# Where the second half's weight and activation tiles lie in SBUF, modulo 512 bytes

## The chip, the cores and the metric

The kernel runs on one core of a Trainium2 chip. The metric is the device time of one execution in microseconds; a profiled execution also leaves a trace with the start and length of each instruction on every engine: TensorE (PE, with its weight loads listed apart as PEld), VectorE (DVE), ScalarE (ACT), GpSimd (POOL) and SyncE (SP, which issues most DMAs).

## The reference, cut to what matters

Two transformer blocks run over 256 tokens of 1024 features, all in float32. The first block mixes, routes each token to two of 32 experts, and normalises. The second block has two layers; each is a feed-forward part, a mixer with two kinds of attention, and another feed-forward part:

```python
def _swiglu(h, w_gate_up, w_down):
    g, u = jnp.split(h @ w_gate_up, 2, axis=-1)
    return (jax.nn.silu(g) * u) @ w_down

for layer in range(DEPTH_2):                       # DEPTH_2 = 2, D_FF = 2816
    x = x + FFN_RES_WEIGHT * _swiglu(_rmsnorm(x, ffn1_norm[layer]), ...)
    x = x + _hybrid_mixer(_rmsnorm(x, mix_norm[layer]), w_in[layer], ...)
    x = x + FFN_RES_WEIGHT * _swiglu(_rmsnorm(x, ffn2_norm[layer]), ...)
return _rmsnorm(x, final_norm)
```

## The kernel before, in words

The second half (the second block, from about 698 us on) is what the change touches. Its weights stream from HBM into nine slots of 128 partitions x 8 KB (`Stream`). The `Feeder` takes half a slot at a time and splits it in two parts: ScalarE writes `hi`, the weight rounded to float32r (line 139), and VectorE writes `lo`, what is left of it (line 152). Each part is a tile of 128 x 1024 float32r, 4096 bytes in a partition. The two parts of one half slot are called a pair here. Six pairs exist (`HB3 = 6`); `fd.pair` hands out the next one, and a pair is written again when TensorE is done with it.

Activations are split in the same way, into tiles of 8192 bytes in a partition: `XH`, `XL` hold the normalised input, `OH`, `OL` the middle of a feed-forward part or the heads' outputs. A product is three matmuls, hi times hi, hi times lo and lo times hi (`mm3`, lines 284 to 287). Each matmul has its own weight load: one operand is loaded into the array first, 128 columns of 4 bytes (512 bytes in a partition; called stationary), the other is streamed past it (called moving). The trace writes `out<-moving,stationary`. There are three kinds in the second half:

- `block` in `ffn` and `feat_block` in `mixer`: the weight part is stationary, the activation tile is moving, 256 columns wide (`o<-XH,whi`). One block is 4 pairs x 24 = 96 matmuls.
- `down` in `ffn`, `skew_last` and the output projection: `OH` or `OL` is stationary, the weight part is moving, 512 columns wide (`g<-whi,OH`). One `down` is 2 pairs x 12 = 24 matmuls.
- `skew_first` and `tok_block`: `XH` or `XL` is stationary, the weight part is moving, 512 columns wide (`g<-whi,XH`).

One step of a feed-forward part is a block and a `down`, so six pairs, and there are 11 such steps in a part. The order of all work is written out by hand.

Tiles of a pool lie one after another in the order in which their tags appear. The two tags of the pool `w3` (line 1309) have six buffers of 4096 bytes each, all multiples of 512, so every weight part starts at one place modulo 512; call it 0. Behind it the pool `work3` begins with a tile of 112 floats (448 bytes, `pad0`) that nothing uses, then `XH`, `XL`, then one of 16 floats (64 bytes, `pad1`), then `OH`, `OL`. So the X tiles start at 448 and the O tiles at 0. Slices of 128 columns move by 512 bytes, and slices of the X and O tiles by 1024 or 512, so these places hold for every matmul.

In the first half, in one pool (`mid`), the tiles `OA`, `OB` and the weight tiles `w` are all 8192 bytes, so they start at one place modulo 512, and so do the nine slots.

Of the kernel before, what the change touches and what calls it, by code (L numbers as in the profile page):

```python
# [10 lines left out]
F32 = mybir.dt.float32  # L11
F32R = mybir.dt.float32r
# [166 lines left out]
def body(tc, A, out, taps=None, stop=None):  # L179
# [3 lines left out]
    with es:  # L183
# [20 lines left out]
        fd = Feeder(nc, st)  # L204
# [91 lines left out]
        def halves(p, names):  # L296

            return [p.tile([128, 8, 256], F32R, name=n, tag=n, bufs=1) for n in names]
# [50 lines left out]
        work = mpool = mid.enter_context(tc.tile_pool(name="mid", bufs=1))  # L349
# [18 lines left out]
        work = p1.enter_context(tc.tile_pool(name="work1", bufs=2))  # L368
        XH, XL = halves(const, ("XH", "XL"))
# [352 lines left out]
        for gi in range(2):  # L722
            for hf in range(2):
                banks = feat_block()
                for c in range(4):
                    n = 4 * hf + c
# [580 lines left out]
        p3 = ExitStack()  # L1307
        HB3 = fd.hb = 6
        w3 = p3.enter_context(tc.tile_pool(name="w3", bufs=fd.hb))
        fd.pair = lambda i: [w3.tile([128, 1024], F32R, name=n) for n in ("whi", "wlo")]  # L1310
        work = p3.enter_context(tc.tile_pool(name="work3", bufs=2))
        fd.order += order2

        work.tile([128, 112], F32, name="pad0", bufs=1)
        XH, XL = halves(work, ("XH", "XL"))
        work.tile([128, 16], F32, name="pad1", bufs=1)
        OH, OL = halves(work, ("OH", "OL"))
        xn = [work.tile([128, 1024], F32, name=f"xn{t}", bufs=1) for t in range(2)]
        junk = work.tile([128, 1024], BF16, name="junk", bufs=1)
        RS = [work.tile([128, 8], F32, name=f"rs{t}", bufs=1) for t in range(2)]  # L1320
# [589 lines left out]
```

## Time and profile before

| | us |
|---|---|
| median of 3 runs | 1706.86 (1705.93 to 1706.91) |
| profiled execution, own time | 1707.14 |
| its span, first to last instruction | 1705.3 |
| PE busy in the span | 1566.1 (92%) |
| PE weight loads busy | 1227.6 (72%) |
| DVE busy | 814.7 (48%) |
| ACT busy | 646.9 (38%) |

The trace gives a matmul's length with its way through the array, so matmuls overlap, and the pace is read from start to start. The granted clock is the share of 2.4 GHz that TensorE got in a stretch.

### The profile page before, as it was taken

To read this page: it belongs to the slowest core of one execution; us is meant where nothing else is said; L and a number is where in the kernel's file an instruction comes from. 1 tells how busy PE (TensorE), PEld (TensorE's weight loads), DVE (VectorE), ACT (ScalarE), POOL (GpSimd) and SP (SyncE) were. 2 spreads that over 40 slices of the span, in tenths; PEclk is the share of its full clock that TensorE was granted. 3 is DMA by queue.
4 is the path that set the end of the run, shared out by engine and by line. 5 is a ranking of instruction groups with operands and counts; after the bars stand their busy time and mean duration, and the time that the engine had idled before them with its cause. 6 is when DMAs were issued, how large, how long until landed. Compare 5 with 4: busy or idle time off the path is not lost.

```text
span 1705.3 us, 24578 instructions
## 1 busy us (share of the span) xinstructions
PE 1566.1 (92%) x10196; PEld 1227.6 (72%) x10196; DVE 814.7 (48%) x1202; ACT 646.9 (38%) x959; POOL 124.7 (7%) x153
## 2 busy tenths in 40 slices
PE   8799997777687876899999999999999999999998
PEld 7789972222222221599989879999899989889997
DVE  5765560000000000765567866555655567765554
ACT  6456420000000100444445655444544455654443
POOL 3430020000000100200003000000000021000000
PEclk9899999988988899899999999999999999999999
DMA  9756679999999999775514555555555514465510
GB/s 335 181 182 240 268 303 420 422 421 421 421 422 420 419 420 376 282 285 185 196 50 161 179 213 198 188 198 177 188 192 195 176 51 158 175 240 192 184 64 26
DMA packets 85893, 418.91 MB, mean 246 GB/s; under 512 B 7552, under 2 KB 7752, under 8 KB 49936
## 3 DMA queue, kind: packets, MB, share of 16 engines
q1 hardware_dynamic: 82112, 407.07, 63.3%
q0 software_dynamic: 3392, 9.17, 2.1%
q8 instruction: 82, 1.34, 0.3%
q10 hardware_dynamic: 272, 1.05, 0.2%
q14 instruction: 35, 0.29, 0.0%
HBM read 414.60 MB, written 2.62 MB: 245 GB/s over the span
## 4 chain that ended last, share of the span: by engine, by line
PE 55%; DVE 3%; DMA 1%; ACT 0%; issue 0%; POOL 0%; POOLq 0%; DVEq 0%; SPq 0%; ACTq 0%
PE g L285 8%; PE g L286 8%; PE g L287 8%; PE o L287 5%; PE o L285 5%; PE o L286 5%; PE a L285 4%; PE a L286 4%; PE a L287 4%; DMA slot<-in_w_down_dram 1%; DVE wlo L152 1%; PE tp L1355 1%; PE fo L1733 0%; PE t L1622 0%; DVE slot L1769 0%
## 5 line engine op out<-in xcount | busy, mean ns | idle before, releaser
L152 DVE TENSOR_TENSOR wlo<-slot,whi 128x1024 fp32r<-128x1024 f32 x298 | 360.3, 1225 | 234.3 <-ACT whi L139 234.0
L139 ACT ACTIVATE whi<-slot 128x1024 fp32r<-128x1024 f32 x300 | 311.2, 1055 | 257.1 <-PE o L286 83.2
L285 PE MATMUL o<-XH,whi 128*128 128x256 f32 x640 | 180.0, 281 | 0.0
L286 PE MATMUL o<-XL,whi 128*128 128x256 f32 x640 | 179.8, 281 | 0.0
L287 PE MATMUL o<-XH,wlo 128*128 128x256 f32 x640 | 179.8, 281 | 0.0
L285 PE MATMUL g<-whi,OH 128*128 128x512 f32 x416 | 165.5, 398 | 0.0
L287 PE MATMUL g<-whi,OL 128*128 128x512 f32 x416 | 162.1, 390 | 0.0
L286 PE MATMUL g<-wlo,OH 128*128 128x512 f32 x416 | 162.0, 390 | 0.0
L285 PE MATMUL a<-XH,whi 128*128 128x256 f32 x512 | 143.9, 281 | 0.0
L286 PE MATMUL a<-XL,whi 128*128 128x256 f32 x512 | 143.9, 281 | 0.0
L287 PE MATMUL a<-XH,wlo 128*128 128x256 f32 x512 | 143.9, 281 | 0.0
L1078 DVE TENSOR_TENSOR eb<-eb,eu 128x512 f32<-128x512 f32 x8 | 5.5, 688 | 259.5 <-PE eu L1074 249.8
L287 PEld LDWEIGHTS o<-XH,wlo 128*128 128x128 f32 x640 | 122.3, 191 | 0.0
L286 PEld LDWEIGHTS o<-XL,whi 128*128 128x128 f32 x640 | 120.6, 188 | 0.6
L285 PEld LDWEIGHTS o<-XH,whi 128*128 128x128 f32 x640 | 120.3, 188 | 0.6
L285 PE MATMUL g<-XH,whi 128*128 128x256 f32 x384 | 113.9, 297 | 0.0
L286 PE MATMUL g<-XL,whi 128*128 128x256 f32 x384 | 106.7, 278 | 0.0
L287 PE MATMUL g<-XH,wlo 128*128 128x256 f32 x384 | 106.7, 278 | 0.0
L287 PEld LDWEIGHTS a<-XH,wlo 128*128 128x128 f32 x512 | 98.3, 192 | 0.0
L286 PEld LDWEIGHTS a<-XL,whi 128*128 128x128 f32 x512 | 96.1, 188 | 0.6
L285 PEld LDWEIGHTS a<-XH,whi 128*128 128x128 f32 x512 | 96.1, 188 | 0.6
L1077 ACT ACTIVATE eb<-eg 128x512 f32<-128x512 f32 x8 | 4.8, 597 | 236.9 <-PE eu L1074 197.3
(520 smaller groups left out, 3469.6 us busy)
## 6 DMA issues: line engine op xcount, KB each, us to landing
slot<-in_gu_dram SPq DMA_DIRECT2D x79, 1024.0 KB, 4.9
slot<-in_w_gate_up_dram SPq DMA_DIRECT2D x45, 1024.0 KB, 19.8
slot<-in_dn_dram SPq DMA_DIRECT2D x40, 1024.0 KB, 5.0
slot<-in_w_in_dram SPq DMA_DIRECT2D x37, 1024.0 KB, 5.2
slot<-in_w_down_dram SPq DMA_DIRECT2D x31, 1024.0 KB, 19.8
ew<-in_w_gate_up_dram SPq DMA_DIRECT2D x31, 1024.0 KB, 19.8
e<-in_w_gate_up_dram SPq DMA_DIRECT2D x15, 1024.0 KB, 19.9
ew<-in_w_down_dram SPq DMA_DIRECT2D x14, 1024.0 KB, 19.8
```

What stands on the lines that cost most here:

```text
L139: self.nc.scalar.activation(hi[:, c], src[:, c], AF.Copy)
L152: self.low.tensor_tensor(lo[:, c], src[:, c], hi.bitcast(F32)[:, c], ALU.subtract)
L285: mm(o, sh, mh, start=start, stop=False, skip_group_check=skip)
L286: mm(o, sh, ml, start=False, stop=False, skip_group_check=skip)
L287: mm(o, sl, mh, start=False, stop=stop, skip_group_check=skip)
L1077: act(esg, g, AF.Silu)
L1078: dve.tensor_tensor(esg, esg, u, ALU.mult)
L1355: nc.tensor.transpose(p[:, i * 128:(i + 1) * 128], src[:, c], ident)
```

## The change

It changes where tiles start and nothing else: no instruction is added, removed or moved. In the pool `w3` each of the six pairs gets tags of its own, and unused tiles ("step") are placed between them: 32 floats (128 bytes) before pair 0, 16 floats (64 bytes) before each other pair, and 16 behind the last. Modulo 512, with 0 as above, pair 0 starts at 128, pair 1 at 192, then 256, 320, 384 and 448. The steps add up to 128 + 5 x 64 + 64 = 512 bytes, as `pad0` and `pad1` did, so `work3` starts at 0 again; its pads are gone, and `XH`, `XL`, `OH`, `OL` all start at 0. Pair `i % 6` is the `i`-th one that the Feeder fills; before, the pool rotated through its six buffers in the same way.

```diff
         w3 = p3.enter_context(tc.tile_pool(name="w3", bufs=fd.hb))
-        fd.pair = lambda i: [w3.tile([128, 1024], F32R, name=n) for n in ("whi", "wlo")]
+        HIGH_LOW = ("whi", "wlo")
+
+        for i in range(HB3):
+            w3.tile([128, 16 if i else 32], F32, name="step", tag=f"step{i}", bufs=1)
+            for n in HIGH_LOW:
+                w3.tile([128, 1024], F32R, name=n, tag=f"{n}{i}", bufs=1)
+        w3.tile([128, 16], F32, name="step", tag="step", bufs=1)
+        fd.pair = lambda i: [w3.tile([128, 1024], F32R, name=n, tag=f"{n}{i % HB3}", bufs=1) for n in HIGH_LOW]
         work = p3.enter_context(tc.tile_pool(name="work3", bufs=2))
         fd.order += order2
-
-        work.tile([128, 112], F32, name="pad0", bufs=1)
-        XH, XL = halves(work, ("XH", "XL"))
-        work.tile([128, 16], F32, name="pad1", bufs=1)
-        OH, OL = halves(work, ("OH", "OL"))
+        XH, XL, OH, OL = halves(work, ("XH", "XL", "OH", "OL"))
```

## Rows read from the trace of the kernel before

**Rows 1.** Page, part 1: busy us and share of each engine.

```profile
PE 1566.1 (92%) x10196; PEld 1227.6 (72%) x10196; DVE 814.7 (48%) x1202; ACT 646.9 (38%) x959; POOL 124.7 (7%) x153
```

**Rows 2.** A window of the second half: busy us (instructions) by engine, granted clock, DMA.

```profile
1000.00:1200.00 200.00, 199.40 (x1357) 183.37 (x1357) 115.42 (x124) 90.63 (x105) 2.63 (x5) 1.00 0.57 199
```

**Rows 3.** Waits of PE, 800 to 1705 us: total us, times, longest.

```profile
PE tp L1355 <- DVE xn L1348: 1.4, 5, 0.3
```

**Rows 4.** Groups by form, PE, 690 to 1705 us: shape, count, busy us, mean ns.

```profile
L285 PE MATMUL o<-XH,whi 128*128 128x256 f32 x640 | 180.0, 281 | 0.0
L285 PE MATMUL g<-whi,OH 128*128 128x512 f32 x416 | 165.5, 398 | 0.0
L285 PE MATMUL a<-XH,whi 128*128 128x256 f32 x512 | 143.9, 281 | 0.0
L286 PE MATMUL g<-XL,whi 128*128 128x256 f32 x384 | 106.7, 278 | 0.0
L285 PE MATMUL g<-whi,XH 128*128 128x512 f32 x64 | 27.1, 424 | 0.0
L285 PE MATMUL o<-whi,XH 128*128 128x512 f32 x64 | 27.1, 423 | 0.0
```

**Rows 5.** Tile whi, 800 to 1705 us: duration ns min/median/max.

```profile
L285 PE MATMUL o<-XH,whi x561: 281/281/281, 800.0 to 1681.4; 128*128 128x256 f32 x187
L285 PE MATMUL a<-XH,whi x448: 281/281/281, 811.5 to 1664.6; 128*128 128x256 f32 x150
L286 PE MATMUL g<-XL,whi x352: 276/276/283, 903.1 to 1536.2; 128*128 128x256 f32 x176
L287 PE MATMUL g<-whi,OL x384: 388/389/398, 806.5 to 1697.8; 128*128 128x512 f32 x192
```

**Rows 6.** Timeline, PE: start us, length; first and 97th matmul of a run.

```profile
1105.44 0.28 PE L285 MATMUL o<-XH,whi 128*128 128x256 f32 x1
...
1116.75 0.39 PE L285 MATMUL g<-whi,OH 128*128 128x512 f32 x1
```

**Rows 7.** Timeline, PE: first and 43rd matmul of a run.

```profile
1027.03 0.28 PE L287 MATMUL g<-XH,wlo 128*128 128x256 f32 x1
...
1031.79 0.28 PE L287 MATMUL g<-XH,wlo 128*128 128x256 f32 x1
```

**Rows 8.** Timeline, PE, first half: first and 97th matmul of a run.

```profile
197.40 0.28 PE L285 MATMUL o<-OB,w 128*128 128x256 f32 x1
...
208.92 0.40 PE L285 MATMUL g<-w,Y 128*128 128x512 f32 x1
```

**Rows 9.** Timeline, PE: first and 24th matmul of a `down`.

```profile
1100.00 0.39 PE L285 MATMUL g<-whi,OH 128*128 128x512 f32 x1
...
1105.21 0.39 PE L287 MATMUL g<-whi,OL 128*128 128x512 f32 x1
```

**Rows 10.** Timeline, PE: first and 19th matmul of a run in `skew_first`.

```profile
1022.09 0.39 PE L287 MATMUL o<-whi,XL 128*128 128x512 f32 x1
...
1026.21 0.39 PE L287 MATMUL o<-whi,XL 128*128 128x512 f32 x1
```

**Rows 11.** Groups by form, ACT and DVE, 800 to 1705 us.

```profile
L139 ACT ACTIVATE whi<-slot 128x1024 fp32r<-128x1024 f32 x265 | 275.4, 1055 | 234.3 <-PE o L286 74.4 <-PE a L286 72.6 <-issue 39.4
L152 DVE TENSOR_TENSOR wlo<-slot,whi 128x1024 fp32r<-128x1024 f32 x266 | 321.4, 1223 | 214.5 <-ACT whi L139 214.2
```

**Rows 12.** Timeline, PE, experts: three matmuls at once; then a group by form.

```profile
686.22 0.60 PE L1096 MATMUL ey<-slot,eb 128*32 128x512 f32 x3
...
L1603 PE MATMUL ro<-slot,eXH 128*128 128x512 f32 x16 | 8.2, 591 | 0.0
```

**Rows 13.** Groups by form, PEld, 790 to 1705 us: weight loads of 128 and 64 columns.

```profile
L285 PEld LDWEIGHTS o<-XH,whi 128*128 128x128 f32 x576 | 108.1, 188 | 0.6
L1735 PEld LDWEIGHTS fo<-PT,slot 128*64 128x64 f32 x32 | 3.9, 137 | 2.2
```

**Rows 14.** Timeline, PEld: a weight load beside the matmul that starts with it.

```profile
1105.44 0.19 PEld L286 LDWEIGHTS o<-XL,whi 128*128 128x128 f32 x1
```

## The prediction

> **What bounds the kernel now.** I read the page's engine totals first: PE is busy for 1566.1 us of the 1705.3 us span, and no other engine passes half [rows 1]. A window of the second half then shows PE busy for 199.4 of 200 us at the full granted clock of 1.00 (2.4 GHz) [rows 2], and the list of PE's waits there has little in it: its longest total is 1.4 us [rows 3]. So in the stretch that the change touches, the end is set by the pace of the matmuls alone. Nothing else there matters unless it makes PE wait.
>
> The pace has to be read from start to start. The same three-matmul product with the same tiles runs at two paces. A whole feed-forward block takes 1116.75 - 1105.44 = 11.31 us for 96 matmuls, 117.8 ns each [rows 6]. A run of 42 in the block of step 1, same shapes and places, takes 4.76 us, 113.3 ns each [rows 7]. The lengths mark the two: 281 ns goes with 117.8, 276 ns with 113.3. In the banks `o` and `a` every one is 281 (minimum, median and maximum agree); in `g` the median is 276 [rows 5]. A third pace stands in the first half, where moving tile and weight part start at one place: 11.52 us for 96, 120.0 ns [rows 8]. The reader is to see that these are steady states, constant over whole runs, with no wait in them and the clock at full.
>
> The wide matmuls have two: with O stationary and the weights at the same place, 23 starts in 5.21 us, 226.5 ns [rows 9]; with X stationary, 64 bytes before the weights, 18 in 4.12 us, 228.9 ns [rows 10]. Each matmul runs beside the weight load of the next, which starts with it [rows 14].
>
> **The change part by part.** No instruction goes, comes or moves, and no DMA or queue is touched. What changes is the distance, modulo 512, between the two tiles that PE reads at once. Weight part minus X is 64 now; it becomes 128, 192, 256, 320, 384 or 448 by pair. Weight part minus O is 0; it becomes the same six. None of these stands in the trace of before, so each cost is bounded by the nearest rows.
>
> (a) *256-wide, weights stationary.* There are 3 x (640 + 512 + 384) = 4608 [rows 4]. In `g` the mean of 278 lies 2/5 of the way from 276 to 281, so some 3/5 of 1152, 690, are at 113.3 and the other 3918 at 117.8. Lower bound: all come to 113.3, 3918 x 4.5 ns = -17.6 us. Upper bound: all come to 120.0, 3918 x 2.2 + 690 x 6.7 = +13.2 us. The value I take: all at 117.8, so +690 x 4.5 ns = +3.1 us. My reason: a moving tile passes 1024 bytes while the weight load passes 512, so modulo 512 the one overtakes the other once in each matmul. At distances 0 and 64 this falls near the start or the end, where the load has not begun or is done; there a clean state (113.3) exists beside a hindered one. At 128 to 448 it falls in the middle of the load each time, so I expect the hindered state always, at the price that the blocks show for it today.
>
> (b) *512-wide, O stationary.* 3 x 416 = 1248 [rows 4]. They leave distance 0 for six others. The one other distance with rows is that of X, 228.9: +2.4 ns x 1248 = +2.9 us, and that I take. Lower bound 0: the shortest length is 388 against a median of 389 [rows 5], so nothing faster is there to go to. Upper bound: the longest length is 398, +9 ns each, +11.2 us.
>
> (c) *512-wide, X stationary.* 3 x (64 + 64) = 384 [rows 4], already in the hindered state; 0.
>
> (d) *Filling the pairs.* A part of whi takes 1055 ns and of wlo 1223 ns, six pairs in a step of 11.3 + 5.4 = 16.7 us: 6 x 1223 = 7.3 us of DVE. ACT's wait before it ends mostly with PE freeing a pair, DVE's with ACT [rows 11]: the fillers wait for PE. If another place made these longer, half a step of slack hides it. Cost 0; they would show only if both doubled.
>
> Sum: 3.1 + 2.9 = +6.0 us on the profiled execution's own 1707.14 (span 1705.3 and 1.8 around it), 1713.1; the median of the runs lies 0.28 lower, so I say 1713. The bounds together: -17.6 to +24.4 on the median, 1689 to 1731.
>
> **The rivals.** *Clean everywhere (faster).* Whatever makes 117.8 of 113.3 needs the two tiles close together, within 64 bytes; from 128 on it is gone. For it: the pace is worst at distance 0 (120.0 [rows 8]), less at 64 (117.8 [rows 6]), and the change keeps exactly these two out. Against it: at 64 both states exist [rows 5], so distance alone doesn't decide. Time: -17.6 + 0 to 2.9, about 1691. It decides if the overtaking in the middle of a load costs nothing.
>
> *Place doesn't set the pace (no change).* The states come from how each run is entered: after `down` without a stall the blocks are at 117.8, after a stall often at 113.3. For it: the experts' matmuls read three slots at the same place at once, and all take 0.60 us, against 591 ns for one such matmul alone [rows 12], so reading at one place need not hurt. Against it: 120.0 and 226.5 each belong to one distance. Time 1707. The Trainium skill states such a rule: "TensorE: Matmul & The Clock Gate", section "Step-by-step: what each phase is for", says that streaming and weight loads have independent read ports, so loading doesn't take bandwidth from the running matmul, and "SBUF — State Buffer", section "SBUF: two separate sides", that PE never waits on anyone. By these the time would stay at 1707; the experts' rows agree, the three paces at one clock and one shape are not explained by them.
>
> *The reader gets stuck behind the load (much slower).* If the moving tile cannot overtake but follows the load until that ends, it runs at the load's rate. Loads of 128 and 64 columns take 188 and 137 ns [rows 13], 0.80 ns a column, so 102 ns for 128 where the moving tile needs 57. That is up to 45 ns lost, half of it over the six distances: 23 ns x (4608 + 1248) = +135 us, 1842. It decides as soon as the meeting place lies well inside the load. Against it: at distance 64, where the meeting comes early, the cost today is 4.5 ns, not 40.
>
> **How the numbers follow.** Forecast (hindered everywhere, +3 to +24 us, own range 1709 to 1731): 0.44. Clean everywhere, 1691: 0.32. No effect, 1707: 0.18. Stuck, 1842: 0.06. The range 1690 to 1731 leaves out the stuck case and the edges. About 0.2% (3.4 us) is what a measurement can tell from no change. Faster: 0.32. Slower: 0.06 and 0.40 of the forecast's 0.44, 0.46. Same: 0.22.
>
> **What would show it.** In the profile after, the lengths of `o<-XH,whi` and `a<-XH,whi`: 281 (forecast, no effect), 276 (clean), 283 or more (upper bound), above 300 (stuck). The median of `g<-XL,whi` should go from 276 to 281, and that of `g<-whi,OH` from 389 to about 392. The lengths should differ between runs of 24 by their pair: six pairs pass in each step, so a feed-forward part uses the same four for every block and the same two for every `down`. The first half must keep its times, and PE's waits must stay near 1.4 us; if they grow, step (d) is wrong. The prediction is wrong if blocks fall below 11.2 us or if the two halves' paces don't move at all.

## The result and the profile after

The changed kernel takes 1716.38 us (median of 4 runs, 1715.06 to 1717.82); the kernel before took 1706.39 beside it (4 runs, 1705.35 to 1706.91). The ratio is 1.006, 95% interval 1.0042 to 1.0077: slower by about 10 us. The profiled execution took 1716.62, its span 1714.8.

First the page's engine totals (busy us, share, instructions), then the window from 1000 to 1200 us (busy us of PE, PEld, DVE, ACT, POOL, then granted clock, DMA share, GB/s), then PE's longest wait from 800 to 1705 us (total, times, longest). They answer to [rows 1 to 3].

```profile
PE 1577.6 (92%) x10196; PEld 1234.1 (72%) x10196; DVE 815.0 (48%) x1202; ACT 646.8 (38%) x959; POOL 124.8 (7%) x153
```

```profile
1000.00:1200.00 200.00, 199.50 (x1349) 182.25 (x1348) 115.27 (x123) 90.89 (x105) 2.63 (x5) 1.00 0.58 202
```

```profile
PE tp L1358 <- DVE xn L1351: 1.2, 5, 0.3
```

PE is busy 11.5 us longer with the same 10196 instructions, and its weight loads (PEld), which run beside the matmuls, 6.5 us longer; the other engines are where they were. The clock in the window is still 1.00, and PE's longest total wait is 1.2 us. So the change is in the pace of the matmuls. The groups by form (shape, count, busy us, mean ns, idle before) and, for the tile `whi`, the durations (min/median/max ns) answer to [rows 4, 5]:

```profile
L285 PE MATMUL o<-XH,whi 128*128 128x256 f32 x640 | 180.0, 281 | 0.0
L286 PE MATMUL g<-XL,whi 128*128 128x256 f32 x384 | 107.8, 281 | 0.0
L285 PE MATMUL g<-whi,OH 128*128 128x512 f32 x416 | 167.0, 401 | 0.0
L285 PE MATMUL g<-whi,XH 128*128 128x512 f32 x64 | 27.2, 426 | 0.0
```

```profile
L285 PE MATMUL o<-XH,whi x562: 276/280/287, 799.8 to 1690.5; 128*128 128x256 f32 x188
L285 PE MATMUL a<-XH,whi x448: 276/280/287, 811.7 to 1673.6; 128*128 128x256 f32 x150
L286 PE MATMUL g<-XL,whi x352: 274/281/287, 904.4 to 1544.1; 128*128 128x256 f32 x176
L287 PE MATMUL g<-whi,OL x380: 388/394/404, 806.6 to 1704.6; 128*128 128x512 f32 x190
```

The one length 281/281/281 of before has become a spread from 276 to 287: the matmuls no longer run at one pace. The mean of `o` is even the same as before (281). Lengths with one minimum, median and maximum marked a steady state; a spread has to be read from start to start. Here is one step of the second feed-forward part, the first start of each pair's run (start us, length):

```profile
1103.43 0.40 PE L285 MATMUL g<-whi,OH 128*128 128x512 f32 x1
1106.19 0.40 PE L285 MATMUL g<-whi,OH 128*128 128x512 f32 x1
1108.96 0.28 PE L285 MATMUL o<-XH,whi 128*128 128x256 f32 x1
1111.81 0.28 PE L285 MATMUL o<-XH,whi 128*128 128x256 f32 x1
1114.63 0.29 PE L285 MATMUL o<-XH,whi 128*128 128x256 f32 x1
1117.49 0.28 PE L285 MATMUL o<-XH,whi 128*128 128x256 f32 x1
1120.31 0.40 PE L285 MATMUL g<-whi,OH 128*128 128x512 f32 x1
```

The `down` takes 1108.96 - 1103.43 = 5.53 us for 24, 230.4 ns each, where 226.5 stood before [rows 9]. The block takes 11.35 us for 96, 118.2 ns, where 117.8 stood [rows 6]. Within it the four pairs take 2.85, 2.82, 2.86 and 2.82 us. They are pairs 4, 5, 0 and 1, at distances 384, 448, 128 and 192: every second one is slower. The next steps of this part repeat these four paces. In the fourth part the blocks use pairs 0 to 3, and there the last pair, at 320, is faster than any of these. Its first start and the start of the next `down` are:

```profile
1620.53 0.28 PE L285 MATMUL o<-XH,whi 128*128 128x256 f32 x1
1623.25 0.39 PE L285 MATMUL g<-whi,OH 128*128 128x512 f32 x1
```

That is 2.72 us for 24, or 113.3 ns each, the fast pace of [rows 7]; in the first part the pair at 320 runs at 117.9.

The first half keeps its pace, 207.94 - 196.42 = 11.52 us for the 96 matmuls of [rows 8], and so do the fillers of [rows 11]:

```profile
196.42 0.28 PE L285 MATMUL o<-OB,w 128*128 128x256 f32 x1
...
207.94 0.40 PE L285 MATMUL g<-w,Y 128*128 128x512 f32 x1
```

```profile
L139 ACT ACTIVATE whi<-slot 128x1024 fp32r<-128x1024 f32 x265 | 275.4, 1055 | 241.5 <-PE o L286 74.4 <-PE a L286 72.6 <-issue 43.3
L152 DVE TENSOR_TENSOR wlo<-slot,whi 128x1024 fp32r<-128x1024 f32 x266 | 321.4, 1223 | 221.9 <-ACT whi L139 221.6
```

**All kinds over the whole second half.** For each kernel I took the mean of the intervals from one matmul's start to the next, over all recorded ones, without those interrupted by a stall (over 135 ns in blocks, 245 ns in the wide ones). Before and after: blocks 117.11 and 118.19 ns, downs 227.35 and 231.75, X stationary 229.67 and 232.01. The sum: 4608 x 1.08 + 1248 x 4.40 + 384 x 2.34 ns = 5.0 + 5.5 + 0.9 = 11.4 us, as much as PE's busy time rose. Between the first X-stationary matmul of the second half and the start of the last run of downs lie 983.2 us before and 993.2 after, 10.0 more; the two profiled executions differ by 9.5 in all. The last run of 72 downs, with 71 intervals, lies behind that stretch and adds 0.4 (71 x 5.5 ns), and the first half was 0.9 shorter in the profile after: 10.0 + 0.4 - 0.9 = 9.5. That leaves 1.0 us of the 11.4 that did not reach the end. Some 0.6 us of it are the 120 interrupted intervals and the matmuls of other kinds in the stretch, which together took 111.7 us before and 111.1 after. The rest is mostly that the sum counts the interrupted intervals at the full difference.

### The profile page after: what moved, and what is told of

It is laid out like the page before. It is cut to its first block, busy times and chain, and to the rows that moved or that the text cites. A ratio compares the mean times of both kernels' runs of the same rounds, so it can differ in the third digit from the quotient of the medians.

```text
span 1714.8 us, 24578 instructions
## 1 busy us (share of the span) xinstructions
PE 1577.6 (92%) x10196; PEld 1234.1 (72%) x10196; DVE 815.0 (48%) x1202; ACT 646.8 (38%) x959; POOL 124.8 (7%) x153
## 4 chain that ended last, share of the span: by engine, by line
PE 56%; DVE 3%; DMA 1%; ACT 0%; issue 0%; POOL 0%; POOLq 0%; DVEq 0%; SPq 0%; ACTq 0%
PE g L285 8%; PE g L287 8%; PE g L286 8%; PE o L287 5%; PE o L285 5%; PE o L286 5%; PE a L285 4%; PE a L287 4%; PE a L286 4%; DMA slot<-in_w_down_dram 1%; DVE wlo L152 1%; PE tp L1358 1%; PE fo L1736 0%; PE t L1625 0%; DVE slot L1772 0%
## 5 line engine op out<-in xcount | busy, mean ns | idle before, releaser
L139 ACT ACTIVATE whi<-slot 128x1024 fp32r<-128x1024 f32 x300 | 311.3, 1055 | 265.0 <-PE o L286 83.2
L286 PEld LDWEIGHTS o<-XL,whi 128*128 128x128 f32 x640 | 120.3, 188 | 0.8
```

What stands on the lines that cost most here:

```text
L139: self.nc.scalar.activation(hi[:, c], src[:, c], AF.Copy)
L286: mm(o, sh, ml, start=False, stop=False, skip_group_check=skip)
```

## The experiments

All kernels below have the instructions of the kernel before, in the same order; only tile places differ. "W - X, W - O" are the distances from X and O up to the weight part, in bytes. The paces are the means defined above; "second half" is the stretch from its first X-stationary matmul to the start of the last downs. The time of one execution also holds a first half that these edits don't touch and that ended between 693.8 and 698.3 us in the profiles, so it moves by some 4 us for reasons of its own; the paces and the second half are the better measure.

| kernel | W - X, W - O | time us | kernel before, beside it | blocks ns | downs ns | X stat. ns | second half us |
|---|---|---|---|---|---|---|---|
| before | 64, 0 | 1706.39 | | 117.11 | 227.35 | 229.67 | 983.2 |
| after | 128 to 448 | 1716.38 | 1706.39 | 118.19 | 231.75 | 232.01 | 993.2 |
| u128_64 | 128, 64 | 1718.16 | 1705.13 | 119.61 | 229.55 | 232.32 | 997.2 |
| u192_128 | 192, 128 | 1713.42 | 1705.13 | 117.37 | 233.11 | 233.00 | 990.8 |
| u256_192 | 256, 192 | 1723.76 | 1705.13 | 119.73 | 233.44 | 228.75 | 1001.2 |
| u320_256 | 320, 256 | 1706.08 | 1705.13 | 117.11 | 227.37 | 229.68 | 983.2 |
| alt256 | 64 / 320, 0 / 256 | 1704.04 | 1704.62 | 117.10 | 227.39 | 229.72 | 983.1 |
| f96_32 | 96, 32 | 1719.08 | 1704.62 | 118.69 | 233.08 | 233.28 | 996.6 |
| f288_224 | 288, 224 | 1715.53 | 1704.62 | 118.33 | 233.28 | 233.21 | 995.5 |
| f160_96 | 160, 96 | 1727.21 | 1704.62 | 119.97 | 233.38 | 233.72 | 1002.9 |
| alt128 | 64 / 192, 0 / 128 | 1693.94 | 1707.10 | 113.68 | 230.66 | 231.25 | 971.2 |
| x128_o0 | 128, 0 | 1717.95 | 1707.10 | 119.69 | 228.67 | 232.58 | 996.6 |
| hilo | whi 64, 0; wlo 128, 64 | 1716.49 | 1707.10 | 118.19 | 231.75 | 231.67 | 993.0 |
| two128 | four pairs 64, 0; two 192, 128 | 1704.72 | 1705.10 | 116.23 | 229.71 | 231.03 | 981.8 |

All but before, after and two128 are one execution each.

### One place for all pairs, four distances

After the result there were three theories: the distance as predicted (from 128 on all alike), the distance's parity in steps of 64 bytes, and the change of place from pair to pair. Four kernels take the kernel before and shift X and O by 64, 128, 192 and 256 bytes:

```diff
-        work.tile([128, 112], F32, name="pad0", bufs=1)
+        work.tile([128, 112 - 16 * k], F32, name="pad0", bufs=1)   # k = 1, 2, 3, 4
         XH, XL = halves(work, ("XH", "XL"))
         work.tile([128, 16], F32, name="pad1", bufs=1)
         OH, OL = halves(work, ("OH", "OL"))
+        work.tile([128, 16 * k], F32, name="pad2", bufs=1)
```

Expected of u128_64 (k = 1):

> All weight parts at one place; weight minus X 128 bytes, weight minus O 64 (before: 64 and 0). Theory 1, distance (the overtaking falls into the middle of the load from 128 on): blocks at 118 to 119 ns a matmul, downs at 231 to 233 as in the changed kernel, time about 1715. Theory 2, only whether the distance is an odd or an even number of 64 bytes counts: blocks at 119 to 120 (even, as pairs 0, 2 and 4 of the changed kernel: 119.1, 119.7, 118.6), about 1716 to 1720. Theory 3, the change costs because the distance alternates from pair to pair, and any one distance is as good as another: blocks 117, downs 227, 1707.

Expected of u192_128 (k = 2):

> All weight parts at one place; weight minus X 192 bytes, weight minus O 128. Theory 1: blocks 118 to 119, downs 231 to 233, about 1715. Theory 2: blocks 116 to 118 (odd, as pairs 1, 3, 5: 117.6, 116.2, 117.7), and if the downs follow it too, they go back to 227 (even, as 0 is): about 1706. Theory 3: 117 and 227, 1707.

Expected of u256_192 (k = 3):

> All weight parts at one place; weight minus X 256 bytes, weight minus O 192. Theory 1: blocks 118 to 119, downs 231 to 233, about 1715. Theory 2: blocks 119 to 120, downs above 230, 1716 to 1720. Theory 3: 117 and 227, 1707.

Expected of u320_256 (k = 4):

> All weight parts at one place; weight minus X 320 bytes, weight minus O 256. Theory 1: blocks 118 to 119, downs 231 to 233, about 1715. Theory 2: blocks about 116 (pair 3 of the changed kernel has 116.2), downs 227 if they follow it: 1702 to 1707. Theory 3: 117 and 227, 1707.

What follows is read from the durations of `whi` in u320_256, then in u256_192 (min/median/max ns, 800 to 1705 us):

```profile
L285 PE MATMUL o<-XH,whi x558: 280/281/282, 799.9 to 1680.2; 128*128 128x256 f32 x186
L285 PE MATMUL g<-whi,OH x384: 388/389/583, 804.8 to 1696.2; 128*128 128x512 f32 x192
```

```profile
L285 PE MATMUL o<-XH,whi x561: 277/283/284, 799.9 to 1697.6; 128*128 128x256 f32 x187
L285 PE MATMUL g<-whi,OH x371: 393/398/587, 806.0 to 1705.0; 128*128 128x512 f32 x186
```

At 320 and 256 everything is as at 64 and 0, to 0.02 ns of the mean: the place counts modulo 256 bytes, not 512. That falls against the first theory, by which 320 and 256 had to be as slow as 128. A change of place can't be what costs either, since uniform places cost up to 18 us. Parity fits the blocks (64 and 192: 117.1 and 117.4; 128 and 256: 119.6 and 119.7) but not the downs: 227.4 at 0, 229.6 at 64, 233.1 at 128, 233.4 at 192.

### Alternating places that are equal modulo 256

```diff
+        for i in range(HB3):
+            if i == 3:
+                w3.tile([128, 64], F32, name="step", tag="step", bufs=1)
+            for n in ("whi", "wlo"):
+                w3.tile([128, 1024], F32R, name=n, tag=f"{n}{i}", bufs=1)
+        slot = lambda i: i % HB3 // 2 + 3 * (i % 2)
+        fd.pair = lambda i: [w3.tile([128, 1024], F32R, name=n, tag=f"{n}{slot(i)}", bufs=1) for n in ("whi", "wlo")]
...
-        work.tile([128, 112], F32, name="pad0", bufs=1)
+        work.tile([128, 48], F32, name="pad0", bufs=1)
```

> Three of the six pairs lie 256 bytes further than the other three, and the order of use goes back and forth between the two groups, so that the place changes from every pair to the next; distances of weights to X 64 and 320, to O 0 and 256. Theory P (the pace goes by the distance modulo 256 bytes, and changing the place from pair to pair costs nothing): all the distances are those of the kernel before, blocks 117.1 ns, downs 227.4, X stationary 229.7, about 1706 us. Rival A (a change of place between neighbouring pairs costs by itself): blocks 118 or more, downs 230 or more, about 1712 to 1716 us.

It runs at the paces of the kernel before in all three kinds. Staggering by itself costs nothing; the distances modulo 256 do.

### Odd multiples of 32 bytes

```diff
-        work.tile([128, 112], F32, name="pad0", bufs=1)
+        work.tile([128, p], F32, name="pad0", bufs=1)   # p = 104 (f96_32), 56 (f288_224), 88 (f160_96)
...
+        work.tile([128, 112 - p], F32, name="pad2", bufs=1)
```

> All pairs at one place, weights 96 bytes from X and 32 from O. Theory P with a step of 64 bytes as its grain: the blocks lie between their paces at 64 and 128 (117.1 and 119.6 ns), the downs between theirs at 0 and 64 (227.4 and 229.6): about 1706 to 1720 us. Theory G (the grain is 32 bytes: a distance of an odd number of 32 bytes is a place of its own): something outside these, the blocks nearer to the undisturbed 113.3 ns (down to 1689 us) or slower than 119.7 (over 1722 us).

> All pairs at one place, weights 288 bytes from X (32 modulo 256) and 224 from O. Theory P with a grain of 64: blocks between their paces at 0 and 64 (119.7 and 117.1 ns), downs between theirs at 192 and 0 (233.2 and 227.4): about 1706 to 1727 us. Theory G (grain 32): outside these on either side.

> All pairs at one place, weights 160 bytes from X and 96 from O. Theory P with a grain of 64: blocks between their paces at 128 and 192 (119.6 and 117.4 ns), downs between theirs at 64 and 128 (229.6 and 232.7): about 1710 to 1725 us. Theory G (grain 32): outside these on either side.

The downs at 32, 96 and 224 stand at 233.1 to 233.4, outside their neighbours on the 64-byte grid (227.4 and 229.6, 229.6 and 233.1, 233.4 and 227.4) in the first case and at an end in the others; the blocks at 32 and 96 lie between their neighbours, at 160 (119.97) a little above. So 32 bytes are a place of their own for the downs, on the slow side. No uniform place tried here beats 64 and 0 in the blocks, the downs or the time.

### Only X moved

```diff
-        work.tile([128, 112], F32, name="pad0", bufs=1)
+        work.tile([128, 96], F32, name="pad0", bufs=1)
...
-        work.tile([128, 16], F32, name="pad1", bufs=1)
+        work.tile([128, 32], F32, name="pad1", bufs=1)
```

> All pairs at one place, 128 bytes from X but still 0 from O: only the blocks and the matmuls with X stationary get a new distance. Theory P, and that the terms add: blocks 119.6 ns (+2.5 x 4608 = 11.5 us), X stationary 232.3 (+1.0), downs still 227.4; about 1715 to 1717 us. Rival (what costs is the distance between X and O, or any change of the layout): the downs slow down too.

The blocks went to 119.69, as expected, and the time to 1717.95, a little above the 1715 to 1717. The downs went to 228.67, where 227.4 was expected, though their distance is unchanged: in each steady `down` the first pair's twelve take 230.3 ns and the second's 226.7. The first intervals behind the block are uneven, 224 to 236 ns, and after about one pair they have settled. The kinds are not quite independent.

### High and low parts apart

```diff
-        fd.pair = lambda i: [w3.tile([128, 1024], F32R, name=n) for n in ("whi", "wlo")]
+        for n in ("whi", "wlo"):
+            for i in range(HB3):
+                w3.tile([128, 1024], F32R, name=n, tag=f"{n}{i}", bufs=1)
+            if n == "whi":
+                w3.tile([128, 16], F32, name="step", tag="step", bufs=1)
+        fd.pair = lambda i: [w3.tile([128, 1024], F32R, name=n, tag=f"{n}{i % HB3}", bufs=1) for n in ("whi", "wlo")]
...
-        work.tile([128, 112], F32, name="pad0", bufs=1)
+        work.tile([128, 96], F32, name="pad0", bufs=1)
```

> All high parts of the weights at one place, 64 bytes from X and 0 from O as in the kernel before; all low parts 64 bytes further, so 128 from X and 64 from O. A block is three matmuls: XH over whi, XL over whi, XH over wlo, and while one runs, the weights of the next are loaded (whi, wlo, whi). Theory L (the moving tile meets the load of the next weights): of the three, XL over whi goes at the pace of 128 bytes (about 119.6 ns to the next start), the two others at that of 64 (117.1). Rival S (a matmul's pace goes by its own stationary tile): XH over wlo is the slow one. Both: blocks 117.9 in the mean (+3.8 us), downs (227.4 + 229.6 + 227.4) / 3 = 228.1 (+0.9), about 1709 to 1711 us. Third: a state carried from one matmul to the next, so that no one of the three stands out.

The intervals behind the three are 118.89 (XH over whi), 119.46 (XL over whi) and 116.21 ns (XH over wlo). By S the third had to be the slowest; it is the fastest, so S falls. L has the slowest right but not the other two, which had to be at 117.1. The sizes missed too: the downs came to 231.75 where 228.1 was expected, and the time to 1716.49 where 1709 to 1711 was. The intervals run from 113 to 124 ns without a period of three: the third reading, a state carried on, is not excluded. The test did not single out the load of the next weights.

### Alternating by 128 bytes: faster than both

The edit is that of alt256 with another step; against alt256:

```diff
-                w3.tile([128, 64], F32, name="step", tag="step", bufs=1)
+                w3.tile([128, 32], F32, name="step", tag="step", bufs=1)
...
-        work.tile([128, 48], F32, name="pad0", bufs=1)
+        work.tile([128, 80], F32, name="pad0", bufs=1)
```

> As alt256, with 128 bytes between the two groups of pairs: weights alternately 64 and 192 bytes from X, 0 and 128 from O. Theory P (each pair goes at the pace of its own distance modulo 256, so that a staggered kernel is the mean over its pairs): blocks (117.1 + 117.4) / 2 = 117.2 ns, downs (227.4 + 233) / 2 = 230.2, X stationary (229.7 + 233) / 2 = 231.4; 4608 x 0.1 + 1248 x 2.8 + 384 x 1.7 ns = 4.7 us above the kernel before, about 1709 to 1710 us. Rival (neighbouring pairs set each other's pace): downs at both distances alike and the blocks away from 117.

It came out 13 us faster than the kernel before beside it, where 1709 to 1710 us was expected. The page's totals, the durations of `whi`, and one step of the timeline (two pairs of downs, a block, the next `down`):

```profile
PE 1554.4 (92%) x10196; PEld 1211.3 (72%) x10196; DVE 814.7 (48%) x1202; ACT 647.0 (38%) x959; POOL 124.6 (7%) x153
```

```profile
L285 PE MATMUL o<-XH,whi x552: 276/276/277, 799.8 to 1667.8; 128*128 128x256 f32 x184
L287 PE MATMUL g<-whi,OL x384: 388/392/403, 802.9 to 1684.6; 128*128 128x512 f32 x192
```

```profile
1093.94 0.39 PE L285 MATMUL g<-whi,OH 128*128 128x512 f32 x1
1096.67 0.40 PE L285 MATMUL g<-whi,OH 128*128 128x512 f32 x1
1099.46 0.28 PE L285 MATMUL o<-XH,whi 128*128 128x256 f32 x1
1102.18 0.28 PE L285 MATMUL o<-XH,whi 128*128 128x256 f32 x1
1104.90 0.28 PE L285 MATMUL o<-XH,whi 128*128 128x256 f32 x1
1107.62 0.28 PE L285 MATMUL o<-XH,whi 128*128 128x256 f32 x1
1110.35 0.39 PE L285 MATMUL g<-whi,OH 128*128 128x512 f32 x1
```

The block's four pairs take 2.72, 2.72, 2.72 and 2.73 us, 113.4 ns a matmul at 64 and at 192 alike: the clean pace of [rows 7], in every steady block. The downs pay: 2.73 us for the pair at 0, 2.79 for the one at 128. In sum 4608 x -3.43 + 1248 x 3.31 + 384 x 1.58 ns = -15.8 + 4.1 + 0.6 = -11.1 us, and the second half is 12.0 shorter. The pace of a pair is thus not the pace of its own distance, since uniform 64 and uniform 192 both run at 117: the theory P of the expectation falls. Of its rival, half came out: the blocks left 117, but the downs at the two distances are not alike. At 64 and 192 blocks have two paces, 113.3 and 117.8.

### What puts the blocks into the fast pace

Against alt128, so that the feed-forward parts see different orders of places:

```diff
-            if i == 3:
+            if i == 4:
...
-        slot = lambda i: i % HB3 // 2 + 3 * (i % 2)
-        fd.pair = lambda i: [w3.tile([128, 1024], F32R, name=n, tag=f"{n}{slot(i)}", bufs=1) for n in ("whi", "wlo")]
+        fd.pair = lambda i: [w3.tile([128, 1024], F32R, name=n, tag=f"{n}{i % HB3}", bufs=1) for n in ("whi", "wlo")]
```

> Only the fifth and sixth of the six pairs lie 128 bytes further, so at 192 from X and 128 from O; the other four are at 64 and 0. In the steady part of the four feed-forward stages the places then come in three patterns: in the first, downs at 0, blocks at 64 64 192 192; in the second and third, downs at 0, blocks at 192 192 64 64; in the fourth, downs at 128 and all blocks at 64. The theory by now: at 64 and 192 a run of blocks has two paces, 113.3 and 117.8 ns, and keeps the one it has; what is open is what puts it into the fast one in alt128. Theory C (a change of the weights' place by 128 bytes inside a run of blocks): the first three stages go to 113.3, the fourth stays at 117.8; 3 x 960 x 4.5 ns = 13 us gained less about 264 downs x 6 ns = 1.6 us in the fourth, 1695 us or a little more where only the half behind the change is fast. Theory E (the downs at 128 ahead of the blocks hand the fast pace on): only the fourth is fast, and the first three are as in the kernel before; 960 x 4.5 = 4.3 us gained, 1.6 lost, about 1704 us. Both at work: about 1691. In each case the downs at 0 stay at 226.7 in the first three stages.

In all, nothing changed (ratio 0.9997, 0.9988 to 1.0007, 10 runs against 13). Inside, two things cancel. A step of the second feed-forward part (downs at 0), then one of the fourth (downs at 128), same kernel:

```profile
1099.33 0.39 PE L285 MATMUL g<-whi,OH 128*128 128x512 f32 x1
1102.10 0.39 PE L285 MATMUL g<-whi,OH 128*128 128x512 f32 x1
1104.82 0.28 PE L285 MATMUL o<-XH,whi 128*128 128x256 f32 x1
...
1116.13 0.39 PE L285 MATMUL g<-whi,OH 128*128 128x512 f32 x1
```

```profile
1547.42 0.40 PE L285 MATMUL g<-whi,OH 128*128 128x512 f32 x1
1550.22 0.40 PE L285 MATMUL g<-whi,OH 128*128 128x512 f32 x1
1553.02 0.28 PE L285 MATMUL a<-XH,whi 128*128 128x256 f32 x1
...
1563.90 0.40 PE L285 MATMUL g<-whi,OH 128*128 128x512 f32 x1
```

In the second part the block takes 1116.13 - 1104.82 = 11.31 us, 117.8 ns, although its places change from 192 to 64 half-way; in the fourth it takes 1563.90 - 1553.02 = 10.88 us, 113.3 ns, with every pair at 64. So theory C fails for these steps, and what theory E forecast came out: the same blocks at the same places take another pace behind other work. The fourth part's blocks stand at the place of the kernel before, where all steady feed-forward blocks take 11.31 us [rows 6]. The price is in its downs: 2.80 us a pair, 233.3 ns. There is a second price that no theory had: the downs at 0 were to stay at 226.7 in the first three parts, but in the second part the first pair takes 1102.10 - 1099.33 = 2.77 us, some 230 ns each, as in x128_o0.

Two things limit this. First, a change of place does go with a change of pace in blocks that no `down` precedes. Such a one, at 192, 192, 64 and 64, is the second block of the second part; the first start of each pair and of the `down` behind it:

```profile
1037.87 0.28 PE L285 MATMUL o<-XH,whi 128*128 128x256 f32 x1
1040.69 0.28 PE L285 MATMUL o<-XH,whi 128*128 128x256 f32 x1
1043.52 0.28 PE L285 MATMUL o<-XH,whi 128*128 128x256 f32 x1
1046.24 0.28 PE L285 MATMUL o<-XH,whi 128*128 128x256 f32 x1
1048.96 0.39 PE L285 MATMUL g<-whi,OH 128*128 128x512 f32 x1
```

Its pairs take 2.82, 2.83, 2.72 and 2.72 us: the slow pace at 192, the fast one at 64. Second, the fourth part was fast before any `down` at 128 had run. Its block ahead of the first `down`, from this start to 1547.42, takes 10.90 us, 113.5 ns:

```profile
1536.52 0.28 PE L285 MATMUL o<-XH,whi 128*128 128x256 f32 x1
```

In alt128, too, the blocks reach the fast pace ahead of the first `down` of each part. So the runs don't show whether downs at 128 put the blocks into the fast pace or only keep them in it.

Theory E's forecast is shown for blocks whose first pair is at 64. It isn't general: in u192_128 the downs at 128 go over into blocks at 192, and those run at 117.8. Yet 192 has the fast pace as well. In the same kernel the block ahead of the second part's first `down` takes 10.88 us, 113.3 ns, all at 192:

```profile
1039.20 0.28 PE L285 MATMUL o<-XH,whi 128*128 128x256 f32 x1
1050.08 0.40 PE L285 MATMUL g<-whi,OH 128*128 128x512 f32 x1
```

## Why the prediction was right, and where it was not

**What bounds the kernel, and step (d).** Right. Waits stayed near 1.4 us (1.2), the fillers took 1055 and 1223 ns as before, and the first half kept its pace.

**Step (b), the downs.** Right in sign and mis-sized: forecast 228.9 ns and +2.9 us, measured 231.75 and +5.5 us, inside the bounds of 0 to +11.2. I took the one other distance that had rows (64), and the uniform kernels show that 64 is the mildest of the others: 229.6 there, 233.1 and 233.4 at 128 and 192.

**Step (c).** X stationary was put at 0 because it was "already in the hindered state"; it cost 0.9 us. There is no one such state: 229.7 at 64, 232.3 at 128, 233.0 at 192.

**Step (a), the blocks: the sum fair, the reason wrong.** Forecast +3.1 us, measured +5.0, because places at 128 and 256 run at 118.5 to 120.3 and not at 117.8. The reason was that the two tiles meet once per matmul modulo 512, and that in the middle of the load only the hindered state exists. The runs show a period of 256 bytes (u320_256, alt256), and at 192, which by that reason had no clean state, a whole block runs at 113.3 (u192_128, from 1039.20 on) and so do the pairs at 192 in alt128. What they show instead, for distances that are multiples of 64: at an odd multiple there are two paces, 113.3 and 117.8, and which one a run takes depends on what ran before it. At an even multiple the paces of the pairs lie between 118.5 and 120.3. At 128 there are two of these as well. A block of u128_64 that no `down` precedes takes 11.39 us, 118.6 ns, and its steady blocks 11.52 us, 120.0 ns:

```profile
1229.77 0.28 PE L285 MATMUL o<-XH,whi 128*128 128x256 f32 x1
1241.16 0.40 PE L285 MATMUL g<-whi,OH 128*128 128x512 f32 x1
```

In the changed kernel even and odd multiples alternate every 24 matmuls, and each pair has its own pace, which repeats from step to step. How the memory or the array makes these paces, the runs don't show.

**How much of it was luck.** The three terms were to add 6.0 us and added 11.4 to PE's work; they were short by 1.9, 2.6 and 0.9 us, all on one side and all within the range. By the reason given, the pairs at 192 in alt128 had to take the slow pace; they took the fast one, and its blocks gained 15.8 us. So the sign came out because half of the changed kernel's pairs lie at even multiples of 64 and most of its odd ones took the slow pace, which the reason given doesn't explain.

**The rivals.** *Clean everywhere* did not happen, but its price was real: alt128 has the clean blocks and gains what was worked out for them (-15.8 us against a bound of -17.6). *Place doesn't set the pace* is refuted as it stood, since uniform shifts other than by 256 bytes lengthen the second half by 7.7 to 19.7 us; yet its mechanism, that the state comes from how a run is entered, has its part at odd multiples, as two128 shows. By the Trainium skill's rule beside that rival ("TensorE: Matmul & The Clock Gate", "Step-by-step: what each phase is for"), loading weights takes no bandwidth from the streaming matmul. As a forecast of 1707 it failed: with the instructions unchanged, the time rose by 10 us. That the load takes something from the stream is not shown by this, since hilo did not single out the load. *Stuck behind the load* did not happen: no kernel's mean interval in blocks is above 120.0.

**What would show it.** The median of `g<-XL,whi` went from 276 to 281 as forecast, and that of `g<-whi,OH` from 389 to 394, where I had named 392. Lengths differ between pairs, as forecast. `o<-XH,whi` gave none of the single lengths that I had listed, but a mixture from 276 to 287.

## What to carry to other kernels

When TensorE runs without a wait, the distance between the stationary and the moving tile in SBUF can still be worth up to 6% of a matmul's pace (here 113.3 against 120.0 ns, 256 columns of float32r with a weight load for each matmul), and it can be set with an unused tile of a few floats. Measure it as start-to-start intervals by kind and stage, since the total hides gains and losses that cancel (two128), and try alternating places too, since the pace of one kind of matmul can depend on the kind that runs before it. Here placing half of the pairs 128 bytes further gave 1693.94 us against 1707.10, one execution of each; I have not repeated it.

## What the runs showed of the hardware that I had not expected

- Places count modulo 256 bytes: (320, 256) equals (64, 0) to 0.02 ns in each of the three kinds.
- The same instructions on the same places have two steady paces: blocks at 64 bytes take 113.3 ns a matmul in the fourth feed-forward part of two128 and 117.8 in the kernel before, each held over whole blocks. What I do not know is which entries lead to which pace: behind downs at 128 the blocks were fast at 64 (two128) but not at 192 (u192_128).
- Downs with the weights at O's own place modulo 256 fall back to 226.7 ns within about one pair (12 matmuls) after any entry seen here; at 128 and 192 the uniform kernels stay at 233.1 to 233.4.
- Not tried: all pairs at 64 from X and 128 from O, which would show whether such downs set the fast pace or only keep it, and moving all three tiles together, which would tell distance from place.
